# Way down of a feed-forward layer: 8 weight blocks on column parts of 344, or 7 block products on parts of 258

## The chip, the core and the metric

The kernel runs on one core of a Trainium2 chip. The number that counts is device microseconds of one execution. Engines that run beside each other: TensorE (PE, with its weight loads as PEld), VectorE (DVE), ScalarE (ACT), GpSimd (POOL) and SyncE (SP), which here issues nearly all DMAs. Each engine works through its own list of instructions in a fixed order; an instruction that waits holds up all that stand behind it on its engine.

## What is computed

One inference step of a one-layer decoder trunk: a mixer (gated linear attention, a gated recurrence, windowed attention), a cross-attention to a memory, and a feed-forward part. The change touches the feed-forward part alone:

```
D_MODEL = 1024; D_FF = 4096            # tokens: 1024 of the prompt and 8 samples, N = 1032
def ffn(x, g, w1, w2):
    h = rmsnorm(x, g) @ w1             # the way up, 1024 -> 4096
    return jnp.square(jax.nn.relu(h)) @ w2     # the way down, 4096 -> 1024
xp = xp + ffn(xp, g_ffn[l], ffn_w1[l], ffn_w2[l])
```

All is float32. The kernel splits each operand into two rounded halves (hi and lo, type fp32r) and makes each product from three matmuls: hi·hi, hi·lo, lo·hi.

## The kernel before, in words

Tokens lie along the columns, features on the 128 partitions. The 1032 tokens are cut into three groups of 344 columns.

**Block products.** A weight matrix is cut into blocks a11, a12, a21, a22; sums of them are S1 to S4. With matching sums of the operand (T1 to T4 beside B11, B21, B22), seven products of blocks do the work of eight. This holds for two column groups against each other, so groups 0 and 1 go by seven products, and group 2 by the four plain blocks (GA and GB2 are its operand). A unit of work thus has eight steps, one per prepared weight block: A11, S2, S1, A12, S3, S4, A21, A22.

**The way up** (`up_unit`, 14 units; the first 2 of 16 pairs go by `pl_cell`) makes a pair of 128-feature rows of h. `h_done` lists what is then to be done with the pair: sums on DVE and stores (`h_store`) of each operand, split into hi and lo by ACT and DVE (`halves`: ACT rounds, DVE takes the rest), into a place of a ring, from where a DMA carries it to the DRAM tensor `hd[c]`. These entries are run two at a time in the steps of the next unit (`bg_run(2)`). The pairs 0 and 1 are done in the same way out of the list `slow`, one entry in each of the last three steps of a unit.

**The way down** (`down_unit`, 16 units: 8 parts c of 512 features, 2 halves of the outputs each) loads the operands of part c from `hd[c]` by `h_load` into rooms in SBUF. Every product has two row blocks (u), two depths (k) and three terms. Its PSUM result is added by DVE to an accumulator (`add_acc`) and to the output tiles XT (`add`). XT[0] to XT[7] hold the residual x already: `x_fill` loads them from the DRAM tensor `xd` at the start of the way down, after which the first sums can be added. At the end `y_half` transposes XT on PE and ACT copies it out.

**Order.** `prep` makes the weight operand `wop` of the step that is five steps ahead (LOOK), from raw weights `wraw` (`unit_raw`, one unit earlier still) or their sums `wsum` (`unit_sums`, on POOL). A scheduler orders each engine's list by priority: PSUM results (LIFT_E) before weight preparation (LIFT_W) before the rest.

All matmuls stand on line 140 (`mm`), all ACT operations of these stages on 160 (`act`), DVE sums on 170 (`tt`).

Of the kernel before, what the change touches and what calls it, by code (L numbers as in the profile page):

```python
# [52 lines left out]
def trunk_step(ctx: ExitStack, tc: tile.TileContext, I: dict, O: list):  # L53
# [7 lines left out]
    psd = ctx.enter_context(tc.tile_pool(name="psd", bufs=1, space=bass.MemoryType.PSUM))  # L61
# [1807 lines left out]
    hd = [dram.tile([18, 128, 2 * GW], F32, name=f"hd{c}") for c in range(NUNIT)]  # L1869
# [6 lines left out]
    RAW, SUM, OPS = {}, {}, {}  # L1876

# [31 lines left out]
    def prep(q):  # L1909

        n, i = divmod(q, 8)
        if n >= len(UNITS):
            return
        with lift(LIFT_W):
            if i == 0:
# [32 lines left out]
    def h_done(p, h):  # L1948
# [19 lines left out]
    def pl_new(p):  # L1968
        c = cells(T("qe"[p], 6 * GW, "hpl"))
        PL[p] = {(f, g): c[3 * f + g] for f in range(2) for g in range(3)}  # L1970

    XOP = {}

    def up_rooms():
# [4 lines left out]
        HC["g"] = cells(F("g", 4 * GW, "gc"))  # L1979

    def st_rooms():
        HC["h"] = [c for i in range(2) for c in cells(F("u", 3 * GW, "hc"))]
        ST["v"] = F("v", 3584, "wsum")
        room = [F("q", 2064, "hst"), ST["v"][:, 2048:]]
        ST["ring"] = [room[i][:, 2 * GW * j:2 * GW * j + 2 * GW] for i, n in ((0, 3), (1, 2)) for j in range(n)]
# [36 lines left out]
    def up_unit(n):  # L2022
# [9 lines left out]
        for i in range(8):  # L2032
# [54 lines left out]
        bg.extend(h_done(p, h))  # L2087
# [3 lines left out]
    def h_place(c, op):  # L2091
        if c % 2 == 0:
            if op in (B11, GA, B21, GB2):
                k = 2 * (B11, GA, B21, GB2).index(op)
                return XH[:, k:k + 2, gs(0)], XL[:, k:k + 2, gs(0)]
            r = (T2, T1, T3, B22, T4).index(op)
        else:
            if op != B11:
                o = (GA, B21, GB2, T2, T1, T3, B22, T4).index(op)
                k, g = 2 * (o % 4), 1 + o // 4  # L2100
                return XH[:, k:k + 2, gs(g)], XL[:, k:k + 2, gs(g)]
            r = 5
        return [v3(x[r // 3], 6)[:, 2 * (r % 3):2 * (r % 3) + 2] for x in (HOP["hs"], HOP["ls"])]

    def h_load(c, op):
        for s, x in enumerate(h_place(c, op)):
            SP.dma_start(x.bitcast(F32), v3(hd[c][9 * s + op], 2))
        HOP[c, op] = h_place(c, op)

    def x_fill(m):  # L2110

        if m > 3:
            t = v3(F("q", 2 * N, "XT"), 2)
        else:
            t = F("u", N, "XT").unsqueeze(1) if m == 3 else v3(F("v", 3 * N, "XT"), 3)
        for k in range(t.shape[1]):
            XT[m + k] = t[:, k]
            SP.dma_start(XT[m + k], xd[m + k])

    def y_half(m, h):  # L2120
        if "y" not in ST:
            ST["y"], ST["ys"] = F("d", 2048, "yo"), F("u", D, "ys")
        yo = v3(ST["y"][:, m % 2 * 1024 + h * 512:m % 2 * 1024 + h * 512 + 512], 4)
        p = psD("yp")
        for t in range(4):
            tr(p[:, t * 128:(t + 1) * 128], XT[m][:, tok(4 * h + t)])
        act(yo, v3(p, 4), AF.Copy)
        c = slice(m * 128, m * 128 + 128)
        SP.dma_start(y_prompt[0].rearrange("(t p) c -> p t c", p=128)[:, 4 * h:4 * h + 4, c], yo)
        if h == 0:  # L2130
            p = psD("yp")
            tr(p[:8, :128], XT[m][:, :NS])
            ys = ST["ys"][:8, m * 128:m * 128 + 128]
            act(ys, p[:8, :128], AF.Copy)
            SP.dma_start(y_sample.rearrange("b o c -> (b o) c")[:, c], ys)

    def down_unit(n):
        _, c, dq = UNITS[n]
        ps = {}
        first, last = c == 0, c == NUNIT - 1  # L2140
        ms = [[4 * dq + 2 * half + u for u in range(2)] for half in range(2)]
        acc = [HC["g"][2 * dq + u] for u in range(2)]

        def add(m, g, p):
            x = XT[m][:, gs(g)]
            with lift(LIFT_E):
                tt(x, x, p, ADD)

        def add_acc(u, p, new=False):
# [197 lines left out]
```

## Time and profile before

| | |
|---|---|
| median of 3 runs | 1396.75 us (1396.65, 1396.75, 1639.47) |
| profiled execution | 1393.74 us, span 1392.0 us |
| granted TensorE clock | 0.984 of full speed, mean |
| way up (14 units) | about 746 to 1037 us |
| way down (16 units) | 1037 us to the end |
| PE busy over the span | 96% |

Rows of the timeline give the start of an instruction, its length, and how many were merged. Rows of groups give count, busy time, mean length and the idle time before them with what ended it. Matmuls overlap on PE, so what one costs in a stream is the distance from start to start, not its length. Rows of a stretch give busy time and count of each engine, the granted clock, the share of time that the DMA engines were busy, and the GB/s.

### The profile page before, as it was taken

The page shows a single profiled execution, that of the slowest core. Times are in us where ns is not written, and L with a number is a line of the kernel's source. Part 1 is how long each engine was busy: PE and PEld are TensorE (multiplying, and loading weights), DVE is VectorE, ACT ScalarE, POOL GpSimd, SP SyncE. Part 2 cuts the span into 40 slices and gives each one's busy share as a digit, 9 for nine tenths or more (in the row PEclk, how much of TensorE's full clock was granted, in tenths as well). Part 3 has the DMA queues.
Part 4 walks back from the last instruction along what each step waited for, and adds up shares of the span by engine and source line. Part 5 has one row for each costly group of instructions (what it writes and reads, how often), then busy time and mean ns, then how long its engine had stood idle before and what let it go on. Part 6 is the DMA issues. An engine that isn't in the chain of part 4 may idle for free.

```text
span 1392.0 us, 23667 instructions
## 1 busy us (share of the span) xinstructions
PE 1332.0 (96%) x8675; PEld 1226.1 (88%) x8675; DVE 992.3 (71%) x2097; ACT 691.7 (50%) x1439; POOL 260.1 (19%) x245
## 2 busy tenths in 40 slices
PE   6999999999997989998999999999998999999998
PEld 5889888777876877786799999999998999999997
DVE  6276787668767664767698888888766666666674
ACT  5265455245476554555566776766663222222232
POOL 3001011300003101020004232243211321321310
PEclk9999999999998899999999999999999999999999
DMA  6114010211101444442243768766689867655403
GB/s 185 46 49 122 9 49 18 67 26 31 47 8 52 140 146 128 141 133 71 71 125 109 243 223 278 251 236 214 215 308 350 309 218 244 214 188 172 158 17 106
DMA packets 197499, 198.91 MB, mean 143 GB/s; under 512 B 27938, under 2 KB 177558, under 8 KB 197368
## 3 DMA queue, kind: packets, MB, share of 16 engines
q1 hardware_dynamic: 196744, 197.11, 43.7%
q8 instruction: 68, 1.11, 0.3%
q0 software_dynamic: 640, 0.30, 0.1%
q14 instruction: 47, 0.39, 0.1%
HBM read 136.83 MB, written 61.60 MB: 143 GB/s over the span
## 4 chain that ended last, share of the span: by engine, by line
PE 81%; DVE 10%; DMA 3%; ACT 3%; issue 1%; SPq 1%; POOL 1%; DVEq 0%; ACTq 0%; POOLq 0%
PE win L140 9%; PE e L140 9%; PE fe L140 8%; PE wo L140 6%; PE c L140 4%; PE d L140 4%; PE ga L140 4%; PE fa L140 4%; PE fd L140 4%; PE f L140 2%; PE v L140 2%; PE gx L140 2%; PE b L140 2%; PE fb L140 2%; PE fc L140 2%; PE fg L140 2%
## 5 line engine op out<-in xcount | busy, mean ns | idle before, releaser
L1906 POOL TENSOR_TENSOR wsum<-wraw 128x512 f32<-128x512 f32 x60 | 82.4, 1376 | 378.4 <-DVE wop L170 285.7
L140 PE MATMUL e<-XH,wop 128*128 128x344 f32 x512 | 133.3, 322 | 4.4 <-DVE XT L170 4.4
L160 ACT ACTIVATE wop<-wraw 128x512 fp32r<-128x512 f32 x120 | 74.4, 628 | 119.9 <-PE c L140 48.8
L140 PE MATMUL win<-XL,wh 128*128 128x344 f32 x384 | 126.6, 330 | 0.0
L140 PE MATMUL win<-XH,wh 128*128 128x344 f32 x384 | 126.1, 329 | 0.2 <-ACT xy L160 0.2
L140 PE MATMUL win<-XH,wl 128*128 128x344 f32 x384 | 125.5, 327 | 0.0
L160 ACT ACTIVATE wh<-ws 128x512 fp32r<-128x512 f32 x130 | 80.2, 628 | 74.7 <-DMA ws<-in_w_out_dram 21.2
L140 PE MATMUL fe<-XH,wop 128*128 128x344 f32 x448 | 114.7, 319 | 0.0
L170 DVE TENSOR_TENSOR wop<-wraw,wop 128x512 fp32r<-128x512 f32 x120 | 86.5, 721 | 38.1 <-ACT wop L160 37.1
L170 DVE TENSOR_TENSOR wl<-ws,wh 128x512 fp32r<-128x512 f32 x130 | 91.4, 715 | 27.2 <-ACT wh L160 21.8
L160 ACT ACTIVATE wop<-wsum 128x512 fp32r<-128x512 f32 x104 | 65.6, 631 | 84.7 <-PE e L140 59.0
L170 DVE TENSOR_TENSOR wop<-wsum,wop 128x512 fp32r<-128x512 f32 x104 | 74.5, 717 | 40.2 <-ACT wop L160 39.4
L140 PEld LDWEIGHTS e<-XH,wop 128*128 128x128 f32 x512 | 91.5, 190 | 4.7 <-issue 4.7
L140 PE MATMUL e<-XL,wop 128*128 128x344 f32 x256 | 82.5, 322 | 0.0
L140 PEld LDWEIGHTS fe<-XH,wop 128*128 128x128 f32 x448 | 78.9, 188 | 0.0
L140 PEld LDWEIGHTS win<-XL,wh 128*128 128x128 f32 x384 | 72.2, 188 | 5.2 <-issue 3.9
L140 PEld LDWEIGHTS win<-XH,wl 128*128 128x128 f32 x384 | 72.3, 188 | 3.6 <-issue 2.7
L140 PEld LDWEIGHTS win<-XH,wh 128*128 128x128 f32 x384 | 72.2, 188 | 3.3 <-issue 1.9
L140 PE MATMUL fe<-XL,wop 128*128 128x344 f32 x224 | 71.4, 319 | 0.0
L160 ACT ACTIVATE hc<-hc 128x344 f32<-128x344 f32 x126 | 61.4, 488 | 19.5 <-DVE hc L170 18.1
L170 DVE TENSOR_TENSOR hst<-hc,hst 128x344 fp32r<-128x344 f32 x79 | 60.5, 767 | 13.6 <-ACT hst L160 12.4
L140 PE MATMUL wo<-XH,wh 128*128 128x344 f32 x192 | 64.0, 334 | 2.5 <-ACT wh L160 2.5
(537 smaller groups left out, 3916.7 us busy)
## 6 DMA issues: line engine op xcount, KB each, us to landing
hd<-hst SPq DMA_DIRECT2D x90, 344.0 KB
wraw<-in_ffn_w_dram SPq DMA_DIRECT2D x60, 512.0 KB
hd<-wsum SPq DMA_DIRECT2D x54, 344.0 KB
XH<-hd SPq DMA_DIRECT2D x48, 344.0 KB
XL<-hd SPq DMA_DIRECT2D x48, 344.0 KB
xoph<-hd SPq DMA_DIRECT2D x24, 344.0 KB
xopl<-hd SPq DMA_DIRECT2D x24, 344.0 KB
ws<-in_w_in_dram SPq DMA_DIRECT2D x24, 256.0 KB
```

The costliest lines, as they stand in the source:

```text
L140: PE.matmul(out, lhsT, rhs, start=start, stop=stop, **kw)
L160: return ACT.activation(out, in_, func, **kw)
L170: return DVE.tensor_tensor(out, a, b, op=op)
L1906: POOL.tensor_tensor(o, a, b, op=op)
```

## The change

On the way down all 1032 tokens go by seven products, with two halves of 516 columns; each matmul takes a quarter, 258 columns. A unit has seven steps (no A21), of 24 matmuls each. The operands are seven instead of nine, each of 516 columns; they lie in a ring of 12 places (RING), and each `h_load` has a time of its own (`at`). The stores go through three places of 1032 columns instead of five of 688. XT starts from the first products (ACT copies them, `new`), and the residual is loaded to a room that has come free (`x_load`) and added later, a half at a time (`x_add`). On the way down PSUM is one pool of four tiles of two banks. The outputs are transposed by `y_out` in the last unit, copied by ACT and DVE half and half. On the way up the step S3 comes after A21.

```diff
+    first_half = ctx.enter_context(ExitStack())
+    psd = first_half.enter_context(tc.tile_pool(name="psd", bufs=1, space=bass.MemoryType.PSUM))
...
-    A11, S2, S1, A12, S3, S4, A21, A22 = range(8)
-    B11, B21, T2, T1, T3, B22, T4, GA, GB2 = range(9)
+
+    A11, S2, S1, A12, S4, A21, S3, A22 = range(8)
+    B11, T2, B21, T1, T3, B22, T4, GA = range(8)
     NPAIR, NPLAIN, NUNIT = DFF // 256, 2, DFF // 512
+    HALF, QU, NOP = N // 2, N // 4, 7
...
+    hd = [dram.tile([2 * NOP, 128, 2 * HALF], F32, name=f"hd{c}") for c in range(NUNIT)]
...
+    def seq(n):
+
+        if UNITS[n][0] == "up":
+            return range(8)
+        return (A11, S2, A12, S1, S4, S3, A22) if n + 1 == len(UNITS) else (A11, S2, A12, S1, S3, S4, A22)
+
+    QUEUE = [(n, i) for n in range(len(UNITS)) for i in seq(n)]
+    BASE = [QUEUE.index((n, A11)) for n in range(len(UNITS))]
...
-        ring_ = ST["ring"] if p < NPAIR - 1 else ST["ring"][:3]
-        st = ring_[ST["n"] % len(ring_)]
+        st = ST["ring"][ST["n"] % len(ST["ring"])]
         ST["n"] += 1
-        hi, lo = f32r(st[:, :GW]), f32r(st[:, GW:])
+        hi, lo = f32r(st[:, :HALF]), f32r(st[:, HALF:])
...
-        a, b, c, d = h[0, 0], h[0, 1], h[1, 0], h[1, 1]
-        return [st(B11, a), sub(a, b, a), st(GA, h[0, 2]), st(T1, a), sub(b, d, b), st(B22, d), sub(d, d, a), st(T2, d),
-                st(B21, c), sub(c, c, d), st(T3, b), st(GB2, h[1, 2]), st(T4, c)]
+        a, b, c, d = (x[:, i * HALF:(i + 1) * HALF] for x in h for i in range(2))
+        return [st(B11, a), sub(a, b, a), st(T1, a), sub(b, d, b), st(T3, b), st(B22, d), sub(d, d, a), st(T2, d),
+                st(B21, c), sub(c, c, d), st(T4, c)]
...
+        ST["q"] = F("q", 4 * HALF, "hst")
+        ST["ring"] = [ST["q"][:, :N], ST["v"][:, 2048:2048 + N], ST["q"][:, N:]]
...
-                for op in {A12: (B11, GA, B21, GB2, T2, T1, T3, B22), S3: (T4,)}.get(i, ()):
+                for op in {S1: (B11, T2), S4: (B21, T1), S3: (T3, B22)}.get(i, ()):
...
+    RING = (("h", 0, 0), ("h", 0, 1), ("x", 4, 0), ("x", 6, 0), ("h", 1, 0), ("h", 1, 1), ("x", 0, 0), ("x", 2, 0),
+            ("x", 0, 1), ("x", 2, 1), ("x", 4, 1), ("x", 6, 1))
+
+    def h_load(c, op):
...
+        kind, k, j = RING[(NOP * c + op) % len(RING)]
...
+        for s, x in enumerate(room):
+            SP.dma_start(x.bitcast(F32), v3(hd[c][NOP * s + op], 2))
+        HOP[c, op] = room
...
+    def x_load(m):
+
+        ST["x", m] = ST["q"][:, m % 2 * N:m % 2 * N + N]
+        SP.dma_start(ST["x", m], xd[m])
+
+    def x_add(m, j):
+        tt(hv(XT[m], j), hv(XT[m], j), hv(ST["x", m], j), ADD)
...
+    def y_rooms(dq):
...
+            XT[3] = F("u", N, "XT")
+            t = F("v", 3 * N, "XT")
+            for m in range(3):
+                XT[m] = t[:, m * N:(m + 1) * N]
+            t = F("u", N, "acc")
+            HC["acc", 0] = [hv(t, u) for u in range(2)]
...
+    def y_out(m, f):
+
+        p = f("yp")
+        for h in range(2):
+            c = slice(512 * h, 512 * h + 512)
+            for t in range(4):
+                tr(p[:, c][:, t * 128:(t + 1) * 128], XT[m][:, tok(4 * h + t)])
+            yo = ST["q"][:, m % 2 * 1024:m % 2 * 1024 + 1024][:, c]
+            if h == 0:
+                act(yo, p[:, c], AF.Copy)
+            else:
+                copy(yo, p[:, c])
+            SP.dma_start(y_prompt[0].rearrange("(t p) c -> p t c", p=128)[:, 4 * h:4 * h + 4, 128 * m:128 * m + 128],
+                         v3(yo, 4))
...
+        psP, psQ = (lambda name, tag=tag: psy.tile([128, 1024], F32, tag=tag, bufs=2, name=name)
+                    for tag in ("pr" if n % 2 else "rp"))
+
+        def pv(p):
+            return v3(p, 2)[:, :, :QU]
+
+        def add(m, j, p, new=False):
+
+            x = v3(hv(XT[m], j), 2)
             with lift(LIFT_E):
                 if new:
-                    act(acc[u], p, AF.Copy)
+                    act(x, pv(p), AF.Copy)
                 else:
-                    tt(acc[u], acc[u], p, ADD)
+                    tt(x, x, pv(p), ADD)
...
-            terms(ps[name, u], [(hi[:, k, 128 * u:128 * u + 128], lo[:, k, 128 * u:128 * u + 128]) for k in range(2)],
-                  [(f32r(x[0])[:, k], f32r(x[1])[:, k]) for k in range(2)], start, stop)
+            for j in range(2):
+                cs = slice(j * QU, j * QU + QU)
+                terms(ps[name, u][:, 512 * j:512 * j + QU],
+                      [(hi[:, k, 128 * u:128 * u + 128], lo[:, k, 128 * u:128 * u + 128]) for k in range(2)],
+                      [(f32r(x[0])[:, k, cs], f32r(x[1])[:, k, cs]) for k in range(2)], start, stop)
...
-                for u in range(2):
                     add_acc(u, ps["a", u], first)
-                for u in range(2):
-                    part("e", u, GA, True, False)
             elif i == A12:
                 for u in range(2):
                     part("a", u, B21, False, True)
-                for u in range(2):
-                    part("e", u, GB2, False, True)
-                for u in range(2):
-                    add(ms[0][u], 0, ps["a", u])
-                    add(ms[0][u], 2, ps["e", u])
+                    add(ms[0][u], 0, ps["a", u], first)
...
+    def at(n, k, fn):
+        loads.setdefault((n, k), []).append(fn)
+
+    d0 = NPAIR - NPLAIN
+    at(d0, 1, lambda: h_load(0, T4))
+    for c in range(1, NUNIT):
+        for op in range(NOP):
+            n, k = divmod(2 * op + 1, NOP)
+            at(*((d0 + 2 * c - 2 + n, k) if c > 1 else (d0 + 1, op)), lambda c=c, op=op: h_load(c, op))
+    for m in range(8):
+        at(d0 + 3 + m, 0, lambda m=m: x_load(m))
+        for j in range(2):
+            at(d0 + 4 + m, 2 + 3 * j, lambda m=m, j=j: x_add(m, j))
+    psy = None
...
-        c, first = u[1], UNITS[n - 1][1] != u[1] or UNITS[n - 1][0] == "up"
-        if c == 0:
-            for m in (0, 3) if u[2] == 0 else (6,):
-                x_fill(m)
-        if first and c + 1 < NUNIT:
-            for j, op in enumerate((B11, GA, B21, GB2, T2, T1, T3, B22, T4)):
-                loads[8 * n + j + 1] = lambda op=op, c=c: h_load(c + 1, op)
+        if n == d0:
+            first_half.close()
+            psy = ctx.enter_context(tc.tile_pool(name="psy", bufs=1, space=bass.MemoryType.PSUM))
+        if u[1] == 0:
+            y_rooms(u[2])
```

DVE, the sums and stores of a pair in the last unit of the way up (hc is h, hst and wsum the places of the ring, gc and fX are sums and PSUM of that unit). Before:

```order
L170 TENSOR_TENSOR hc<-hc 128x344
L170 TENSOR_TENSOR hst<-hc,hst 128x344 x2
L170 TENSOR_TENSOR wop<-wsum,wop 128x512
L170 TENSOR_TENSOR hst<-hc,hst 128x344
L170 TENSOR_TENSOR wsum<-hc,wsum 128x344
L170 TENSOR_TENSOR hc<-hc 128x344
L170 TENSOR_TENSOR wsum<-hc,wsum 128x344
L170 TENSOR_TENSOR wop<-wraw,wop 128x512
L170 TENSOR_TENSOR gc<-fb,gc 128x344
L170 TENSOR_TENSOR wop<-wraw,wop 128x512
L170 TENSOR_TENSOR gc<-fc,gc 128x344
```

and with the change:

```order
L171 TENSOR_TENSOR hc<-hc 128x516
L171 TENSOR_TENSOR hst<-hc,hst 128x516
L171 TENSOR_TENSOR hc<-hc 128x516
L171 TENSOR_TENSOR wsum<-hc,wsum 128x516
L171 TENSOR_TENSOR hst<-hc,hst 128x516
L171 TENSOR_TENSOR wop<-wsum,wop 128x512
L171 TENSOR_TENSOR gc<-fb,gc 128x344
L171 TENSOR_TENSOR wop<-wraw,wop 128x512
L171 TENSOR_TENSOR gc<-fc,gc 128x344
L171 TENSOR_TENSOR wop<-wraw,wop 128x512
L171 TENSOR_TENSOR wsum<-hc,wsum 128x516
L171 TENSOR_TENSOR hc<-hc 128x516
```

Sums and stores are fewer and wider; what reads PSUM stays as it was.

SP, from the last unit of the way up into the first of the way down (hd_4480 is hd[0], hd_4481 is hd[1], hd_4487 is the last; wraw the weights of the unit after next). Before:

```order
L2107 DMA xopl<-hd_4480 128x688
L1946 DMA hd_4487<-hst 128x2x344
L2107 DMA xoph<-hd_4480 128x688
L2107 DMA xopl<-hd_4480 128x688
L1946 DMA hd_4487<-wsum 128x2x344 x2
L2118 DMA XT<-xd 128x1032 x2
L1946 DMA hd_4487<-hst 128x2x344
L1893 DMA wraw<-in_ffn_w_dram 128x2x512 x2
L1946 DMA hd_4487<-hst 128x2x344 x2
L2107 DMA xoph<-hd_4481 128x688
L2107 DMA xopl<-hd_4481 128x688
L1946 DMA hd_4487<-hst 128x2x344
```

and with the change:

```order
L2117 DMA xoph<-hd_4480 128x1032
L2117 DMA xopl<-hd_4480 128x1032
L2117 DMA xoph<-hd_4480 128x1032
L2117 DMA xopl<-hd_4480 128x1032
L1957 DMA hd_4487<-hst 128x2x516
L1905 DMA wraw<-in_ffn_w_dram 128x2x512 x2
L1957 DMA hd_4487<-wsum 128x2x516
L2117 DMA XH<-hd_4480 128x2x516
L2117 DMA XL<-hd_4480 128x2x516
L1957 DMA hd_4487<-hst 128x2x516 x2
L1957 DMA hd_4487<-wsum 128x2x516
L2117 DMA XH<-hd_4481 128x2x516
```

The loads of part 1 (hd_4481) stand behind the last stores but two instead of among them, and no XT is loaded; the raw weights stand behind the loads of part 0 in both.

ACT, the first unit of the way down, from the results of its first product on. Before:

```order
L160 ACTIVATE gc<-ga 128x344 x2
L160 ACTIVATE wop<-wraw 128x512 x3
L160 ACTIVATE hst<-hc 128x344
L160 ACTIVATE wop<-wsum 128x512 x2
L160 ACTIVATE hst<-hc 128x344 x2
L160 ACTIVATE wop<-wraw 128x512
L160 ACTIVATE wop<-wsum 128x512
L160 ACTIVATE hst<-hc 128x344
```

and with the change:

```order
L161 ACTIVATE gc<-a 128x516 x2
L161 ACTIVATE wop<-wraw 128x512
L161 ACTIVATE hst<-hc 128x516
L161 ACTIVATE wop<-wraw 128x512
L161 ACTIVATE XT<-a 128x516 x2
L161 ACTIVATE wop<-wsum 128x512
L161 ACTIVATE XT<-c 128x516 x2
L161 ACTIVATE wop<-wraw 128x512
L161 ACTIVATE hst<-hc 128x516
L161 ACTIVATE wop<-wsum 128x512
L161 ACTIVATE XT<-c 128x516
```

Between the weight preparations there are now copies of PSUM (XT<-a, XT<-c) that were sums on DVE before.

## Rows read from the trace of the kernel before

**Rows 1.** page, part 1: engine, busy us (share of the span), instructions

```profile
PE 1332.0 (96%) x8675; PEld 1226.1 (88%) x8675; DVE 992.3 (71%) x2097; ACT 691.7 (50%) x1439; POOL 260.1 (19%) x245
```

**Rows 2.** stretches: one unit of the way up, one of the way down

```profile
833.00:853.80 20.80, 20.80 (x134) 20.80 (x133) 17.69 (x30) 14.12 (x32) 6.01 (x4) 1.00 0.87 284
...
1181.20:1202.10 20.90, 20.90 (x134) 20.79 (x133) 14.20 (x28) 5.08 (x8) 5.55 (x4) 1.00 0.38 123
```

**Rows 3.** chain that ended last: start, length, what

```profile
1038.94 1.90 PE e L140 x12
...
1059.85 1.92 PE e L140 x12
1066.98 7.65 DMA XT<-xd
...
1086.70 1.91 PE e L140 x12
...
1212.05 1.90 PE e L140 x12
...
1295.62 1.90 PE e L140 x12
```

**Rows 4.** stretches around that wait (columns as in Rows 2)

```profile
1070.00:1075.00 5.00, 1.32 (x9) 1.02 (x7) 1.73 (x3) 0.79 (x2) 0.00 (x0) 1.00 1.04 399
1075.00:1080.00 5.00, 4.27 (x19) 4.30 (x20) 3.40 (x8) 0.00 (x0) 0.00 (x0) 0.66 1.04 399
```

**Rows 5.** timeline of PE: matmuls of 256 columns in a stream

```profile
120.75 0.40 PE L140 MATMUL mkv<-mhl,wh 128*128 128x256 f32 x2
...
126.44 0.40 PE L140 MATMUL mkv<-mhl,wh 128*128 128x256 f32 x2
...
171.99 0.28 PE L140 MATMUL v<-wh,XL 128*128 128x256 f32 x1
...
173.78 0.29 PE L140 MATMUL v<-wh,XL 128*128 128x256 f32 x1
```

**Rows 6.** groups of DVE on the way up, 746 to 1037 us

```profile
L170 DVE TENSOR_TENSOR hst<-hc,hst 128x344 fp32r<-128x344 f32 x72 | 54.4, 756 | 12.3 <-ACT hst L160 11.1
L170 DVE TENSOR_TENSOR hc<-hc 128x344 f32<-128x344 f32 x54 | 44.6, 825 | 1.2 <-ACT hc L160 0.5
L170 DVE TENSOR_TENSOR wop<-wsum,wop 128x512 fp32r<-128x512 f32 x57 | 42.0, 739 | 15.6 <-ACT wop L160 15.3
L170 DVE TENSOR_TENSOR wop<-wraw,wop 128x512 fp32r<-128x512 f32 x56 | 41.7, 744 | 4.7 <-ACT wop L160 4.1
L170 DVE TENSOR_TENSOR wsum<-hc,wsum 128x344 fp32r<-128x344 f32 x47 | 28.5, 606 | 9.5 <-ACT wsum L160 8.9
L170 DVE TENSOR_TENSOR hc<-fd,gc 128x344 f32<-128x344 f32 x28 | 14.3, 510 | 0.2 <-PE fd L140 0.2
```

**Rows 7.** groups of DVE in one unit of the way down

```profile
L170 DVE TENSOR_TENSOR wop<-wsum,wop 128x512 fp32r<-128x512 f32 x4 | 2.8, 692 | 1.8 <-ACT wop L160 1.8
```

**Rows 8.** waits on the way up, 746 to 1037 us: total, times, longest

```profile
ACT hst L160 <- DMA hd<-hst: 6.4, 5, 1.5
ACT wsum L160 <- DMA hd<-wsum: 5.2, 3, 3.4
```

**Rows 9.** waits at the start of the way down, 1037 to 1100 us

```profile
PE e L140 <- DVE XT L170: 4.4, 1, 4.4
...
ACT hst L160 <- DMA hd<-hst: 3.3, 4, 1.6
DVE XT L170 <- DMA XT<-xd: 2.9, 4, 1.9
```

**Rows 10.** stretch of the first unit of the way down (columns as in Rows 2)

```profile
1037.00:1057.00 20.00, 20.00 (x128) 19.89 (x127) 15.20 (x27) 9.14 (x18) 4.34 (x5) 1.00 0.96 339
```

**Rows 11.** timeline of ACT and SP at the end

```profile
1386.98 1.08 ACT L160 ACTIVATE yo<-yp 128x512 f32<-128x512 f32 x2 [0.60 <-PE yp L146]
...
1387.60 0.92 SPq L2129 DMA_DIRECT2D out_dram<-yo  x2
```

More of the change, by code (lines that the diff above doesn't have):

```diff
@@ L2105, in h_load @@
[L2105 to L2113, printed above, removed]
-        else:
[L2115 to L2135, printed above, removed]
@@ new lines, in hv @@
+    def hv(x, j):
+        return x[:, j * HALF:(j + 1) * HALF]
+    def x_load(m):
[4 more added lines that the diff above has]
+    def y_rooms(dq):
+        if dq:
+            for m in (4, 6):
+                t = F("q", 2 * N, "XT")
+                XT[m], XT[m + 1] = t[:, :N], t[:, N:]
+            HC["acc", 1] = [HC["gt"][:, u * HALF:(u + 1) * HALF] for u in range(2)]
+        else:
+            XT[3] = F("u", N, "XT")
[4 more added lines that the diff above has]
+            HC["acc", 0] = [hv(t, u) for u in range(2)]
@@ L2137, in down_unit, with ys_out @@
+    def ys_out(ms, f):
+        p = f("ysp")
+        n = 128 * len(ms)
+        for i, m in enumerate(ms):
+            tr(p[:8, i * 128:i * 128 + 128], XT[m][:, :NS])
+        ys = HC["gt"][:8, :n] if ms[0] == 0 else HC["gt"][:8, 1032:1032 + n]
+        act(ys, p[:8, :n], AF.Copy)
+        SP.dma_start(y_sample.rearrange("b o c -> (b o) c")[:, 128 * ms[0]:128 * ms[0] + n], ys)
     def down_unit(n):
@@ L2139, in down_unit @@
         ps = {}
-        first, last = c == 0, c == NUNIT - 1
+        first, last, end = c == 0, c == NUNIT - 1, n + 1 == len(UNITS)
         ms = [[4 * dq + 2 * half + u for u in range(2)] for half in range(2)]
[L2142 to L2149, printed above, removed]
+        acc = HC["acc", dq]
+        psP, psQ = (lambda name, tag=tag: psy.tile([128, 1024], F32, tag=tag, bufs=2, name=name)
+                    for tag in ("pr" if n % 2 else "rp"))
@@ L2150, in add_acc @@
+        def pv(p):
+            return v3(p, 2)[:, :, :QU]
+        def add(m, j, p, new=False):
+            x = v3(hv(XT[m], j), 2)
             with lift(LIFT_E):
                 if new:
-                    act(acc[u], p, AF.Copy)
+                    act(x, pv(p), AF.Copy)
                 else:
-                    tt(acc[u], acc[u], p, ADD)
+                    tt(x, x, pv(p), ADD)
+        def add_acc(u, p, new=False):
+            a = v3(acc[u], 2)
+            with lift(LIFT_E):
+                if new:
+                    act(a, pv(p), AF.Copy)
+                else:
+                    tt(a, a, pv(p), ADD)
@@ L2161, in banks @@
         def banks(f, name):
             for u in range(2):
-                ps[name, u] = f(name)[:, :GW]
-        for i in range(8):
-            q = 8 * n + i
+                ps[name, u] = f(name)
+        for k, i in enumerate(seq(n)):
+            q = BASE[n] + k
             prep(q + LOOK)
             bg_run(2)
-            load = loads.get(n * 8 + i)
-            if load:
-                load()
+            for fn in loads.get((n, k), ()):
+                fn()
             hi, lo = OPS.pop(q)
@@ L2185, in down_unit @@
                     part("a", u, B21, False, True)
-                for u in range(2):
-                    part("e", u, GB2, False, True)
-                for u in range(2):
-                    add(ms[0][u], 0, ps["a", u])
-                    add(ms[0][u], 2, ps["e", u])
+                    add(ms[0][u], 0, ps["a", u], first)
+                if end:
+                    for m in (0, 1):
+                        y_out(m, psP)
             elif i == S2:
-                banks(psD, "b")
+                banks(psQ, "b")
                 for u in range(2):
@@ L2196, in down_unit @@
                     if last:
-                        for m, g in ((ms[0][u], 1), (ms[1][u], 0), (ms[1][u], 1)):
-                            add(m, g, acc[u])
+                        for m, j in ((ms[0][u], 1), (ms[1][u], 0), (ms[1][u], 1)):
+                            with lift(LIFT_E):
+                                tt(hv(XT[m], j), hv(XT[m], j), acc[u], ADD)
+                if end:
+                    for m in (2, 3):
+                        y_out(m, psQ)
             elif i == S1:
-                banks(psD, "c")
+                banks(psQ, "c")
                 for u in range(2):
                     part("c", u, T1, True, False)
-                    add(ms[1][u], 1, ps["c", u])
+                    add(ms[1][u], 1, ps["c", u], first)
             elif i == S3:
-                banks(psC, "d")
+                banks(psP, "d")
                 for u in range(2):
@@ L2211, in down_unit @@
                     part("c", u, B22, False, True)
-                    add(ms[0][u], 1, ps["c", u])
-            elif i == A21:
-                banks(psB, "e")
-                for u in range(2):
-                    part("e", u, GA, True, False)
-                for m in ms[0] * last:
-                    y_half(m, 0)
-                    y_half(m, 1)
+                    add(ms[0][u], 1, ps["c", u], first)
+                if end:
+                    for m in ms[0]:
+                        y_out(m, psQ)
+                    ys_out(range(6), psQ)
             else:
@@ L2222, in down_unit @@
                     part("d", u, T4, False, True)
-                    add(ms[1][u], 0, ps["d", u])
-                for u in range(2):
-                    part("e", u, GB2, False, True)
-                    add(ms[1][u], 2, ps["e", u])
-                    if last:
-                        y_half(ms[1][u], 0)
-        for m in ms[1] * last:
-            y_half(m, 1)
+                    add(ms[1][u], 0, ps["d", u], first)
+                if end:
+                    for m in ms[1]:
+                        y_out(m, psP)
+                    ys_out(range(6, 8), psQ)
     def w1_blk(f):
@@ L2303, in trunk_step @@
     run_steps()
-    slow.extend(h_done(0, PL[0]) + h_done(1, PL[1]))
+    slow.extend(h_done(0, PL["t", 0]) + h_done(1, PL["t", 1]))
+    def at(n, k, fn):
[11 more added lines that the diff above has]
+    psy = None
     for n, u in enumerate(UNITS):
```

43 lines of the change are left out of this document (15 added, 28 removed).

## The prediction

> **What bounds the kernel.** I read the page's busy shares first: PE works through 96% of the span, DVE through 71% [rows 1]. The share alone would not do, so I took stretches of one unit each. On the way up and on the way down PE is busy without a gap and at full clock, while DVE has 17.7 of 20.8 us on the way up and 14.2 of 20.9 on the way down, ACT 14.1 and 5.1 [rows 2]. So each unit lasts as long as its matmuls. The chain of waits gives the period of a down unit: the same product starts at 1212.05 and, four units later, at 1295.62, which is 20.89 us [rows 3]. A unit has 132 matmuls of 344 columns (11 products of 12), so one costs 158.3 ns. The one break is early: between 1059.85 and 1086.70 the chain needs 26.85 us for one unit, 5.96 more than the period, and the step in between is the load of XT [rows 3]. PE stood 4.4 us for a sum on DVE that waited for that load [rows 9], and after it the granted clock of a 5 us stretch was 0.66, that is, a part of it at 1.2 instead of 2.4 GHz [rows 4].
>
> **The matmuls.** The change takes out 132 matmuls of 344 columns a unit and puts in 7 × 24 = 168 of 258. By columns that is 43,344 for 45,408, only 4.5% less, so everything hangs on what a narrower matmul costs. The kernel has streams of 256 columns, with a weight load for each matmul as here: 48 in 5.69 us from 120.75 to 126.44, that is 118.5 ns, and 15 in 1.79 us, that is 119.3 [rows 5]. From 256 to 344 columns a column costs (158.3 − 118.9)/88 = 0.45 ns, so two more make 119.8; I take 120.0. Bounds: 118.7 if cost goes with columns (158.3 × 258/344), 122.5 if all above the bare column time at 2.4 GHz (158.3 − 143.3 = 15.0) is fixed per matmul. A unit becomes 168 × 120.0 = 20.16 us and 16 units give back 16 × (20.89 − 20.16) = **11.7 us** (5 to 15.2). The gain is gone at 20.89/168 = 124.3 ns.
>
> **The load of XT.** It is no longer waited for: ACT copies the first products into XT, and the residual is added in units 4 to 11 of the way down, when nothing waits for it. That gives back the excess of **6.0 us**. The sums of the residual are two of 516 columns a unit, about 0.7 us each; with 7 splits and 14 sums of PSUM DVE then has 7 × 0.69 + 16 × 0.70 = 16.0 of 20.2 us, so PE hides them.
>
> **What comes late instead.** Two places at the start of the way down are close. (a) Four loads of part 0 can't be issued before the fifth product of the last up unit is done with their rooms, 84 of its 132 matmuls or 13.3 us into it. Behind them on SP and in the DMA queue stand a store, four more loads, a store, and then the raw weights of the unit after next: 10 × 0.528 + 1.05 = 6.3 MB. A full queue moved 339 to 399 GB/s [rows 4, 10], so they land 16 to 19 us later, 8 to 11 us into the first down unit. ACT's list has the rounding of these weights ahead of its copy of the third product (XT<-a), whose banks the fifth needs at 4 × 24 × 0.120 = 11.5 us. (b) The loads of T4 come after that, 1.6 MB and 4 to 5 us later, 12 to 16 us into the unit; they are needed at 17.3, and PE's list puts half a product of the next unit ahead. One unit later the raw weights stand behind the last stores, again about as early as needed. I take **1 us** for all this; nothing below, 8 us above (the old wait again with its clock, and a little more). The loads of part 1, which filled the queue at the old wait, now have a unit to themselves.
>
> **The way up.** Its matmuls stay. DVE gets 11 sums and stores of 516 for 13 of 344, ACT 7 roundings for 9. A sum that reads PSUM, which nothing disturbs, takes 510 ns for 344 columns [rows 6] and a split of 512 takes 692 [rows 7], so one of 516 is about 0.70: 11 × 0.70 − 13 × 0.51 = 1.1 us more per unit, and 22 × 0.70 − 26 × 0.51 = 2.1 us once for the pairs in the list `slow`. DVE has 3.1 us of idle time per unit to hide it; if that cover were gone, each us would be one of PE. The ring has three places for five. For the last pair the old kernel used three as well, with the DMA queue full, and ACT waited 3.3 us for it in all [rows 9], against 11.6 us over the whole way up with five [rows 8]. ACT is idle 6.7 us a unit, and weights are made five steps ahead, so a wait of that size is hidden. I take **1 us** for the way up; bounds 0 and 30, the latter below.
>
> **The end.** Before and after, 72 transposes stand between the last products, and the path behind the last matmul is a sum, transposes, a copy, a DMA of 256 KB [rows 11]. The sum is 0.2 us longer, one of the two copies goes to DVE, and in the last unit transposes wait for banks that DVE frees after six sums of 0.7 us. I take **0.5 us**, bounds −1 and 2.
>
> **Sum.** 1393.74 − 11.7 − 6.0 + 1 + 1 + 0.5 = 1378.5 us for the profiled execution. The two runs that agree, the median one among them, lie 3.0 us above it, so I forecast **1381 us**, 1.1% less than before.
>
> **Rivals.**
> - *DVE bounds the way up (slower).* For: its sums of two SBUF operands take 606 to 825 ns against 510 with a PSUM operand [rows 6], at the times when POOL works on its sums. If the disturbed lengths grow with the columns, 173 such entries at 127.5 us in all become 1.5 × 11/13 of that, 34 us more over 14 units, and `slow` 4 more. Of the 43 us idle, 39 are waits for ACT (11.1, 15.3, 4.1 and 8.9 [rows 6]), which stay. Then some 34 us come through: 1381 − 1 + 34 = 1414 us. It decides once the extra work of a unit passes the 0.3 us that is truly free. Against: these waits for ACT stand where DVE is ahead of its work, and shrink when it falls behind. Chance 0.06. The Trainium skill, "SBUF — State Buffer", section "Who interferes with whom", says that a DVE instruction with two SBUF inputs and a GpSimd one that reads SBUF exclude each other for their whole length; by that rule the wait goes with POOL's instructions, which the change leaves alone, and the rival falls away. The trace agrees in that only those with two SBUF operands are long (825 against 510 ns).
> - *A new wait at the start of the way down.* If (a) or (b) comes 3 us later than I work out, PE stops, and the clock falls as it did before [rows 4]: 6 to 8 us, 1387 to 1389. Chance 0.10.
> - *The change doesn't do what it says.* At 124.3 ns or more for a matmul of 258 columns, since two streams into two banks and 36 more weight loads a unit are new: 1393 and up. Against it stand rows of 118.5 and 119.3 ns for nearly that width. Chance 0.04.
> - *The bare column time.* If the 15 ns above the columns were not paid in this stage, 258 columns would cost 107.5 ns, a unit 18.06 us, and 16 units 45 us less than before: 1381 − 34 = 1347. The rows speak against it: at 256 columns 12 ns remain. Chance 0.02. The Trainium skill, "TensorE: Matmul & The Clock Gate", section "Back-to-back issue gap", gives N/2.4 + 2.5 ns for a warm matmul by itself, an estimate of 110 ns here and about 1354 us. By that rule 344 columns would take 146 ns; the trace has 158.3, so the measurement decides.
>
> The forecast has 0.78. **Range** 1372 to 1394: it takes in the bounds of the matmul's price (3.5 us less to 6.7 more), the new wait, and the case of no gain where that begins; it leaves out most of the DVE rival and the bare column time, 0.06 + 0.02, and some 0.1 of the edges. **Chances**: 2% is about what a measurement of this kernel can tell from no change; faster by more needs less than 1368.8, which the bare column time and a sliver of the forecast give: 0.03. Slower by more needs over 1424.7, the DVE rival at its worst: 0.02. Within: 0.95.
>
> **What would show it.** Right: twelve matmuls of 258 columns in 1.44 us; a down period of 20.2 us; no wait of PE for XT, and the residual's loads far from the chain; an up period of 20.8 us still. Wrong: 1.49 us or more for twelve; DVE over 20 us in an up unit with PE waiting for its sums (gc<-fb, hc<-fd); PE idle 10 to 20 us into the way down with ACT or DVE held by a DMA; a stretch there at a lower clock.

## The result, and the profile after

The changed kernel takes **1405.69 us** (median of 5 runs, 1404.23 to 1409.29) against 1396.65 for the kernel before on the same chip: a ratio of 1.0086, 95% interval 1.0059 to 1.0114. (One run of the kernel before, of 1639.47 us, was in a slower state; the ratio leaves it out.) The change makes the kernel 0.9% slower. The forecast was 1381 us, range 1372 to 1394: wrong in sign, and outside its range.

The page's first part of the changed kernel, to set beside [rows 1]:

```profile
PE 1326.3 (94%) x9251; PEld 1219.1 (87%) x9251; DVE 1017.0 (72%) x1993; ACT 686.8 (49%) x1393; POOL 255.1 (18%) x245
```

Shares of the whole span hide what happened. Two stretches show it, one unit of the way up and one of the way down (start and end, length, busy time and count of PE, PEld, DVE, ACT, POOL, granted clock, DMA share, GB/s), to set beside [rows 2]:

```profile
790.70:813.30 22.60, 21.10 (x133) 20.81 (x133) 18.72 (x28) 15.33 (x31) 5.95 (x4) 1.00 0.71 258
1110.20:1130.40 20.20, 20.20 (x171) 20.20 (x170) 13.98 (x20) 4.92 (x8) 5.35 (x5) 1.00 1.04 397
```

The way down is as forecast: a unit in 20.2 us, PE without a gap. The way up is not: its unit is now 22.6 us, and PE is idle in 1.5 of them.

The chain of waits of the changed kernel gives both periods: `fd` is A22's first product on the way up, `a` a product of the way down.

```profile
768.25 2.15 PE fd L141 x12
...
790.24 0.44 DVE hc L171
790.72 2.16 PE fd L141 x12
...
812.80 0.44 DVE hc L171
813.28 2.15 PE fd L141 x12
...
1110.24 2.87 PE a L141 x24
...
1130.37 2.86 PE a L141 x24
...
1150.50 2.88 PE a L141 x24
```

From 1110.24 to 1150.50 two units take 40.26 us, that is 20.13 for one and 119.8 ns for a matmul of 258 columns; I had 20.16 and 120.0. From 790.72 to 813.28 an up unit takes 22.56 us for 20.81 before, and a DVE instruction stands in the chain just ahead of each `fd`. The waits of PE between 748 and 1072 us (total, times, longest):

```profile
PE fd L141 <- DVE hc L171: 22.1, 13, 3.7
PE a L141 <- ACT hc L161: 0.5, 1, 0.5
```

In the kernel before PE waited for nothing between 746 and 1037 us, and between 1037 and 1100 for XT alone [rows 9]. Its stretch from 748 to 1036 us has PE busy all the time:

```profile
748.00:1036.00 288.00, 288.00 (x1829) 288.00 (x1828) 239.00 (x381) 198.69 (x426) 85.32 (x58) 1.00 0.68 232
```

The account of the profiled executions goes by the first matmul of the way up and of the way down. Before:

```profile
745.50 0.32 PE L140 MATMUL fa<-XH,wop 128*128 128x344 f32 x1
...
1036.89 0.32 PE L140 MATMUL ga<-XH,wop 128*128 128x344 f32 x1
```

and with the change:

```profile
748.72 0.32 PE L141 MATMUL fa<-XH,wop 128*128 128x344 f32 x1
...
1069.64 0.39 PE L141 MATMUL a<-xoph,wop 128*128 128x258 f32 x1 [0.55 <-ACT hc L161]
```

Up to the way up it is +3.2 us, with the same work, which is the distance of one execution from another; the way up takes 320.9 us for 291.4, **+29.5**; the way down 337.7 us for 355.1, **−17.4**. Together that is +15.3, from 1392.0 to 1407.3. (The profiled execution of the changed kernel is the slowest of its five, so the medians lie only 9 us apart.) Of the 29.5 us, 22.6 are the waits above; the rest, some 7 us, is a lower clock after two of them and about 0.26 us a unit that do not show as waits (a unit with a wait of 1.39 us takes 22.46 for 20.81).

One of the thirteen places, in the timeline of the changed kernel (in brackets the idle time before, and what ended it):

```profile
785.31 0.69 DVE L171 TENSOR_TENSOR wop<-wsum,wop 128x512 fp32r<-128x512 f32 x1
...
787.45 1.62 POOL L1918 TENSOR_TENSOR wsum<-wsum,wraw 128x512 f32<-128x512 f32 x1
...
787.85 1.78 DVE L171 TENSOR_TENSOR wop<-wraw,wop 128x512 fp32r<-128x512 f32 x1
...
788.06 0.32 PE L141 MATMUL fd<-xoph,wop 128*128 128x344 f32 x1
...
789.01 0.32 PE L141 MATMUL fe<-XH,wop 128*128 128x344 f32 x1
...
789.55 0.68 DVE L171 TENSOR_TENSOR hpl<-hpl 128x516 f32<-128x516 f32 x1
790.16 0.50 DVE L171 TENSOR_TENSOR hc<-fd,gc 128x344 f32<-128x344 f32 x1
...
790.72 0.43 PE L141 MATMUL fd<-XH,wop 128*128 128x344 f32 x1 [1.39 <-DVE hc L171]
```

S3's product into the bank fd ends at 788.06 + 0.32 us. The next product into the same bank is A22's, and it may begin only when DVE has read S3's result (`hc<-fd,gc`). PE's list has six matmuls to fe in between, 0.95 us, and then PE stands. DVE has two instructions ahead of the read: a split of 512 columns that takes 1.78 us, while GpSimd sums, instead of 0.69 as two lines up, and a difference of 516 columns. So the read ends 2.34 us after the product (0.95 + 1.39). In the kernel before, S4 and A21 stood between S3 and A22; its chain of waits has them as 24 matmuls:

```profile
757.04 1.89 PE fd L140 x12
758.93 1.89 PE fg L140 x12
760.81 1.88 PE fe L140 x12
762.69 1.90 PE fd L140 x12
```

There the read had 3.76 us, from 758.93 to 762.69. Twice the clock fell after the wait as well. After 2.35 us of idle time (before 859.16) and after 3.65 (before 952.85) the 20 us stretch has a granted clock of 0.91, part of it at 1.2 instead of 2.4 GHz; after waits of 1.39 it stays at 1.00:

```profile
840.00:860.00 20.00, 17.65 (x112) 17.36 (x111) 16.60 (x25) 13.91 (x29) 4.34 (x4) 1.00 0.79 275
860.00:880.00 20.00, 20.00 (x119) 20.00 (x118) 13.51 (x21) 12.66 (x26) 4.12 (x4) 0.91 0.66 237
...
940.00:960.00 20.00, 16.35 (x95) 16.06 (x94) 13.97 (x21) 10.66 (x24) 7.49 (x5) 0.91 0.48 172
960.00:980.00 20.00, 18.61 (x118) 18.32 (x118) 15.38 (x22) 11.66 (x24) 5.83 (x4) 1.00 0.65 234
```

### The profile page after: what moved, and what is told of

It is laid out like the page before. It is cut to its first block, busy times and chain, and to the rows that moved or that the text cites. A ratio compares the mean times of both kernels' runs of the same rounds, so it can differ in the third digit from the quotient of the medians.

```text
span 1407.3 us, 24488 instructions
## 1 busy us (share of the span) xinstructions
PE 1326.3 (94%) x9251; PEld 1219.1 (87%) x9251; DVE 1017.0 (72%) x1993; ACT 686.8 (49%) x1393; POOL 255.1 (18%) x245
## 4 chain that ended last, share of the span: by engine, by line
PE 73%; DVE 14%; ACT 5%; DMA 3%; issue 3%; SPq 1%; POOL 0%; DVEq 0%; ACTq 0%; POOLq 0%
PE win L141 9%; PE a L141 7%; PE d L141 7%; PE c L141 7%; PE wo L141 6%; PE fe L141 4%; PE b L141 3%; PE fa L141 3%; PE fd L141 2%; PE v L141 2%; PE f L141 2%; PE gx L141 2%; PE fb L141 2%; PE fc L141 2%; PE wmo L141 2%
## 5 line engine op out<-in xcount | busy, mean ns | idle before, releaser
L161 ACT ACTIVATE wop<-wraw 128x512 fp32r<-128x512 f32 x104 | 65.3, 628 | 118.5 <-PE b L141 31.3
L171 DVE TENSOR_TENSOR wop<-wraw,wop 128x512 fp32r<-128x512 f32 x104 | 93.5, 899 | 27.8 <-ACT wop L161 24.7
L171 DVE TENSOR_TENSOR wop<-wsum,wop 128x512 fp32r<-128x512 f32 x104 | 80.7, 776 | 17.4 <-ACT wop L161 15.0
L141 PE MATMUL a<-XH,wop 128*128 128x258 f32 x352 | 67.6, 283 | 0.0
L141 PE MATMUL wo<-XH,wl 128*128 128x344 f32 x192 | 64.1, 334 | 1.0 <-DVE wl L171 0.9
L141 PE MATMUL wo<-XL,wh 128*128 128x344 f32 x192 | 63.0, 328 | 0.0
L141 PE MATMUL d<-XH,wop 128*128 128x258 f32 x320 | 60.8, 282 | 0.0
```

The lines of the kernel that those rows point to most:

```text
L141: PE.matmul(out, lhsT, rhs, start=start, stop=stop, **kw)
L161: return ACT.activation(out, in_, func, **kw)
L171: return DVE.tensor_tensor(out, a, b, op=op)
```

## Experiments

The theory (A): the new place of S3 next to A22 makes PE wait for DVE's read of fd. The rivals: (B) DVE has too much to do, in any order; (C) the ring of three places holds ACT and so DVE; and later (E) GpSimd's hold on DVE, (F) the width of 516 itself. All ratios are to the kernel before, run on the same chip.

**1. The changed kernel with the old up order.**

```diff
         if UNITS[n][0] == "up":
-            return range(8)
+            return (A11, S2, S1, A12, S3, S4, A21, A22)
...
-                for op in {S1: (B11, T2), S4: (B21, T1), S3: (T3, B22)}.get(i, ()):
+                for op in {S1: (B11, T2), S4: (B21, T1, T3, B22)}.get(i, ()):
```

> The changed kernel with the order of the eight products on the way up as it was before (S3, S4, A21, A22 at its end; the first four late loads of part 0 all issued after S4). Theory A, the order: in the changed kernel A22 follows S3 directly and adds to the bank fd that DVE has not yet read, so PE waits 1.4 to 3.7 us in each of 13 units (22.1 us) and the clock falls in two of them; the way up took 320.8 us for 291.2. With the old order 24 matmuls stand between, the up period is 20.8 us again, the way up 291 to 293 us, and the time 1405.7 - 29 = 1376 to 1379 us. Theory B, the amount of work on DVE: the wider sums and stores and the ring of three places make DVE late in any order; PE then waits at some other product, the way up stays over 305 us and the time over 1390 us.

1391.19 us, ratio 0.9965 (0.9951 to 0.9979). The way up takes 302.0 us: 19 of the 29.5 are gone, 10.6 stay. Neither forecast holds alone. (Here S3 overwrites a part of T4's operand before it is stored: the first 516 columns of the lower row reach into the 344 that S3 writes. The order of the change writes them later; run 5 stores them earlier.)

**2. The kernel before with the new up order alone** (steps S4, A21, S3, A22; T3's operand is overwritten before its store).

```diff
+    UP = (A11, S2, S1, A12, S4, A21, S3, A22)
...
-        for i in range(8):
-            q = 8 * n + i
+        for j, i in enumerate(UP):
+            q = 8 * n + j
```

> The kernel before with only the new order of the products on the way up (S4, A21, S3, A22 at its end); sums, stores, ring and the whole way down stay. Theory A, the order: the waits of fd for DVE come here too, 12 to 14 of them, 1 to 2 us each, and the time rises by 15 to 30 us to 1412 to 1427 us. Theory B, the amount of work on DVE: narrower sums and a ring of five leave DVE in time, no wait of PE at fd over 0.3 us, and the time stays at 1393 to 1400 us.

1416.44 us, ratio 1.0155 (1.0138 to 1.0172): theory A. Stores of 344 columns and a ring of five do not save it. The waits of PE between 748 and 1050 us:

```profile
PE fd L140 <- DVE hc L170: 14.2, 12, 1.7
```

A thirteenth, of 1.18 us, ends at 1052.37, still on the way up, which takes 310.5 us, 19.1 more than before.

**3. The changed kernel, A22 adding to fe first.**

```diff
-                terms(ps["fd"], w, XOP[T4], False, True)
                 terms(ps["fe"], w, XOP[GA][4:], False, True)
+                terms(ps["fd"], w, XOP[T4], False, True)
```

> The changed kernel, but A22 adds its twelve products to fe ahead of its twelve to fd. That leaves the order of the eight steps and every operation, and puts 1.89 us of matmuls between S3's product and the bank fd's next use. Theory A, the order: the waits of 1.4 to 2.3 us shrink to 0 to 0.5 us each and the clock does not fall; the way up takes 292 to 298 us for 320.8, the time is 1377 to 1384 us. Theory B, the amount of work on DVE: DVE stays late, PE waits elsewhere (gc<-fb, hc<-fg or in the next unit), time over 1395 us.

1394.61 us, ratio 0.9994 (0.9982 to 1.0006). Twelve matmuls now cover the read, 1.89 us, and the shortest waits fall from 1.39 to 0.45 us: 1.89 + 0.45 is 2.34 again, the time that DVE needs. The forecast of 0 to 0.5 us holds for 6 of the 12; the others last 0.7 to 1.9:

```profile
PE fd L141 <- DVE hc L171: 9.3, 12, 1.9
```

After the longest of them, 1.93 us, the clock falls (0.66 in the next 5 us). The way up takes 307.9 us, 13 less than with the change but more than the 292 to 298 that theory A gave, and the time lies above its 1377 to 1384: twelve matmuls are too little cover. Theory B fails too: behind 748 us PE waits nowhere else but for 2.28 us ahead of the first product of the way down.

**4. The changed kernel without GpSimd's block sums on the way up.**

```diff
+        if UNITS[n][0] == "up":
+            SUM[n] = {S1: a21, S2: a11, S3: a11, S4: a12, A11: a11, ...}
+            return
```

> The changed kernel without GpSimd's four sums of weight blocks in each unit of the way up (left out: S1 to S4 use blocks of W1 as they are). The order stays. In the trace of the changed kernel DVE's split of 512 columns just ahead of the read of fd takes 1.78 us instead of 0.67 while GpSimd sums. Theory A in its plain form, the order and one split and one difference that DVE's list has ahead of the read: with the split at 0.67 us each wait is 1.1 us shorter, 0.3 to 0.8 us a unit is left, and the way up takes 295 to 303 us. Theory A', it is the dependency alone (matmul end, signal, read, signal): the waits stay at 1.4 us. Theory C, GpSimd's hold on DVE is the whole cause: no wait is left, 291 to 293 us.

1380.47 us in one run. Of the gain 9 us lie ahead of the way up, whose first matmul comes at 739.4 us for 748.7; run 9, with the same edit, has it at 746.2, so this part is not shown to come from the edit. PE's waits on the way up are two, for 13, with the order as it was changed:

```profile
PE fd L141 <- DVE hc L171: 4.0, 2, 2.1
```

The way up takes 301.6 us, in theory A's range of 295 to 303, but not in the way that it said. The units without a wait take 20.89 to 21.06 us, 0.1 to 0.25 more than before, so each loses less than A's 0.3 to 0.8. The rest is in the two waits, 1.83 and 2.14 us, and the lower clock after each (0.66 in the next 5 us). The second falls beside GpSimd's sums for the way down, which this run keeps; the first begins about 8 us after a row of four of them, and what held DVE there is not shown.

So the order alone costs little in most units: it takes away the cover, and GpSimd's sum, which makes the split ahead of the read 1.1 us longer, makes that felt in nearly every unit.

**5. The old order, with the pair's stores done by the fifth step.** Run 1 and

```diff
-            bg_run(2)
+            bg_run(3 if k == 4 else 2)
```

> The changed kernel with the old order of the products on the way up, and the last of the eleven sums and stores of the pair before run at the fifth step, ahead of S3's new sum (in the order that the change replaced, the 516 columns of the lower row hold half of what S3 writes, so they have to be stored before it). Theory A, the order is two thirds of the loss and the rest is something else: as the run with the old order alone, 1387 to 1392 us, with 3 to 6 waits of PE left. Theory B, the old order without that detail was what was still slow: 1377 to 1381 us.

1388.47 us, ratio 0.9957 (0.9942 to 0.9972), faster than both kernels, with six waits of PE left on the way up: theory A. The way up takes 301.2 us. With runs 1 and 2 that makes a square: old order and stores of 344 columns 291.4 us; new order alone +19.1; the 516 columns and their ring alone +9.8; both +29.5. The two add up. What the 9.8 are, the next runs ask. In this kernel PE waits six times on the way up, 6.2 us, and 1.9 at the first product of the way down:

```profile
PE fd L141 <- DVE hc L171: 5.2, 5, 1.7
PE a L141 <- ACT hc L161: 1.9, 1, 1.9
PE fg L141 <- DVE gc L171: 1.0, 1, 1.0
```

The worst place, DVE and GpSimd from 924 us on:

```profile
924.28 1.76 POOL L1918 TENSOR_TENSOR wsum<-wraw 128x512 f32<-128x512 f32 x1
...
924.91 1.69 DVE L171 TENSOR_TENSOR hc<-hc 128x516 f32<-128x516 f32 x1
...
926.00 1.75 POOL L1918 TENSOR_TENSOR MKV<-wraw,wsum 128x512 f32<-128x512 f32 x1
...
926.52 1.79 DVE L171 TENSOR_TENSOR hst<-hc,hst 128x516 fp32r<-128x516 f32 x1
...
927.70 1.76 POOL L1918 TENSOR_TENSOR wsum<-wraw,wsum 128x512 f32<-128x512 f32 x1
...
928.23 1.78 DVE L171 TENSOR_TENSOR wsum<-hc,wsum 128x516 fp32r<-128x516 f32 x1
...
929.93 0.68 DVE L171 TENSOR_TENSOR wop<-wraw,wop 128x512 fp32r<-128x512 f32 x1
```

In this row each DVE instruction with two operands in SBUF lasts about as long as one of GpSimd's; once GpSimd is done, 0.68 us. `MKV` belongs to the first unit of the way down: its sums had come forward to here.

**6. Five places in the ring, old order.**

```diff
+        more = F("q", 4 * HALF, "hst")
-        ST["ring"] = [ST["q"][:, :N], ST["v"][:, 2048:2048 + N], ST["q"][:, N:]]
+        ST["ring"] = [ST["q"][:, :N], ST["v"][:, 2048:2048 + N], ST["q"][:, N:], more[:, :N], more[:, N:]]
```

> The kernel of the old order and early stores with five places of 1032 columns in the ring for the stores, where the change has three (the room of a residual tile that nothing uses then). With three places and the old order ACT waited 22.1 us for stores to land on the way up, against 11.6 in the kernel before, and PE four times (6.9 us) between 850 and 940 us, when DMA was busy 0.77 to 0.84 of the time. Theory C, the ring holds what is left: ACT waits under 5 us, PE's waits from 748 to 1036 us go, 6.9 us of them and about 2 us of lower clock, 1379 to 1383 us. Theory D, DVE's own amount of work holds it: ACT waits less but PE's waits stay, 1387 to 1392 us.

1394.18 us, ratio 0.9997 (0.9984 to 1.0009). ACT's waits for stores fall from 26.8 us (run 5, on the way up) to 2.9, and the way up from 301.2 to 300.4 us: theory C falls. PE still waits three times there, 4.1 us in all, and after the longest of these, 1.93 us, the clock falls (0.66 in the next 5 us). The whole got slower than in run 5 because the new places lie where XT begins later, so that ACT's first copy into XT waits for the last stores to land:

```profile
1067.38 1.09 ACT L161 ACTIVATE XT<-c 128x516 f32<-128x516 f32 x2 [6.57 <-DMA hd<-hst]
...
1068.04 0.58 PE L141 MATMUL c<-xoph,wop 128*128 128x258 f32 x1 [8.41 <-ACT XT L161]
```

**7. The same, the first product of the way down in other banks.**

```diff
+            psy.tile([128, 1024], F32, tag="p", bufs=2, name="first")
```

> As the run with five places, and the first product of the way down is moved to the other four banks of PSUM. In the old order PE waited 2.3 us for ACT's read of the last fe before the first product of the way down, and the clock of the next 5 us was 0.66. If the bank is what it waits for, this wait goes: 3 to 4 us less than with five places alone, 1375 to 1380 us. If another wait stands there at once (DVE's read of the last fd, or an operand's load), no change.

1396.23 us, ratio 1.0003 (0.9988 to 1.0017); the wait of that product is 1.92 us as in run 6. Whether the edit moved it to other banks is not shown, so this is inconclusive.

**8. Five places in the changed kernel's own order** (the edit of run 6).

> The changed kernel in its own order with five places in the ring. Theory A, in this order the wait is for DVE's read of fd and the ring has no part in it (ACT waited only 3.7 us for stores): within 2 us of the changed kernel, 1403 to 1408 us, 12 to 14 waits at fd. Theory C, the ring makes DVE late there too: 1385 to 1398 us.

1422.63 us, ratio 1.0194 (1.0175 to 1.0213), slower than either theory gave. A wait of 8.1 us for XT's place comes here as well, and at fd PE waits 22.2 us in 11 places; the way up takes 325.1 us for 320.9. More room in the ring does not shorten the waits, as theory A said.

**9. Run 5 without GpSimd's sums on the way up** (the edit of run 4).

> The kernel of the old order and early stores, without GpSimd's sums of weight blocks on the way up (left out: S1 to S4 use blocks of W1 as they are). In its trace with the sums PE waits six times for DVE between 825 and 937 us (6.2 us) and 1.9 us at the first product of the way down; around 921 to 930 us five of GpSimd's sums stand in a row, and each of DVE's instructions with two operands in SBUF takes 1.7 to 1.8 us for 0.69. Theory E, GpSimd's hold on DVE is what is left of the loss: all six waits go, the way up takes 291 to 294 us for 301.2. Theory F, the 516 columns themselves make DVE late: 298 to 301 us.

The way up takes 293.5 us, and of all waits the one at the first product of the way down is left, 1.92 us. Theory E; the width of 516 by itself costs nothing that PE sees on the way up (1380.65 us in one run). With runs 4 and 5 this makes a second square: the new order costs 19.7 us of the way up beside GpSimd's sums (320.9 for 301.2) and 8.1 without them (301.6 for 293.5). So a good half of the order's cost comes only with GpSimd (by one execution of each kernel).

**10. Run 5, the last stores four a step.**

```diff
-            bg_run(3 if k == 4 else 2)
+            bg_run(4 if n == NPAIR - NPLAIN - 1 else 3 if k == 4 else 2)
```

> The kernel of the old order and early stores, with the stores of the last but one pair run four a step in the last up unit, so that they are done three steps earlier. If the first product of the way down waits 1.9 us because ACT's read of the last fe is queued behind a store whose sum on DVE is late, this wait and about 1.5 us of lower clock after it go: 1384 to 1387 us. If GpSimd's first sums for the way down hold DVE there, no change, 1387 to 1390 us.

1389.19 us, ratio 0.9965 (0.9955 to 0.9976), with the same wait of 1.92 us: not the stores.

**11. Run 5, block sums of the up units on DVE.**

```diff
-            POOL.tensor_tensor(o, a, b, op=op)
+            if n < NPAIR - NPLAIN:
+                tt(o, a, b, op)
+            else:
+                POOL.tensor_tensor(o, a, b, op=op)
```

> The kernel of the old order and early stores, with the four sums of weight blocks of each up unit on DVE and not on GpSimd. That gives DVE 4 x 0.68 = 2.7 us more a unit and takes GpSimd's four instructions of 1.3 to 1.8 us away. Theory E, GpSimd's hold on DVE: the waits between 825 and 937 us go, the way up takes 292 to 296 us, the time is 1379 to 1384 us. Theory F, DVE has too much work: PE's waits grow, the way up takes 303 us or more, 1390 us or more.

**1377.56 us**, ratio 0.9885 (0.9870 to 0.9900), a little below theory E's 1379 to 1384. The stretch from 748 to 1036 us, first of run 5, then of this run:

```profile
748.00:1036.00 288.00, 281.81 (x1780) 280.26 (x1779) 236.66 (x340) 193.21 (x386) 84.65 (x55) 1.00 0.69 241
```

```profile
748.00:1036.00 288.00, 286.91 (x1820) 286.63 (x1818) 245.56 (x397) 202.90 (x396) 11.49 (x7) 1.00 0.73 253
```

DVE is busy 9 us longer, and PE waits for it no more on the way up, which takes 293.5 us, as in run 9. What made DVE late was not how much it had to do (theories B and F) but that GpSimd's sums stopped it at the wrong moments (E).

**12. The same for the first two units of the way down as well, with the edit of run 10.**

```diff
-            if n < NPAIR - NPLAIN:
+            if n < NPAIR - NPLAIN + 2:
```

> As the run with the sums on DVE, also for the first two units of the way down, and with the early last stores. Theory E: also the 1.9 us at the first product of the way down and its lower clock go, 2 to 4 us less than with the sums on DVE for the way up alone: 1376 to 1381 us. If that product waits for the banks in any case: as that run.

**1375.17 us**, ratio 0.9872 (0.9859 to 0.9886): the lowest, though its interval overlaps with that of run 11, and by the ratios some 30 us below the changed kernel. The way up takes 292.3 us. The wait at the first product of the way down is not gone, as theory E had it, but is 0.79 us for 1.92, and the clock of the next 5 us is 1.00 for 0.66:

```profile
PE a L141 <- ACT hc L161: 0.8, 1, 0.8
```

## Why the prediction was wrong

**The step that failed** is the way up: "Its matmuls stay", and with them, I took it, its 20.8 us a unit, with 1 us in all for DVE, ACT and the ring. It measured +29.5 us. That this lies just inside the bounds that I had given (0 and 30) is luck: the 30 came from the rival below, whose mechanism is another. The text on the change says that S3 comes after A21, and the prediction never priced it, though the matmuls staying does not make their dependences stay: I looked at how long DVE was busy, and not at how long each of its reads may take before the same bank is needed again. That time fell from 24 matmuls to 6, from 3.76 to 0.95 us, for a read that ends 2.34 us after the product. The rows of before would have told a part of it: a read of 0.51 us [rows 6] behind one split of 0.69 [rows 7] needs 1.2 us, 0.25 more than 0.95, which is about what a unit loses in run 4; the rest comes with GpSimd's hold on the split. Runs 2 and 5 size the two parts: 19 us the order, 10 us the 516 columns, each beside GpSimd's sums. Without these sums (runs 4 and 9) they are 8.1 and 2.1 us.

**The matmuls: right.** 119.8 ns for 258 columns, forecast 120.0; 16 × (20.89 − 20.13) = 12.2 us for 11.7. The estimate of 110 ns from the Trainium skill, "TensorE: Matmul & The Clock Gate", section "Back-to-back issue gap", is not what these streams show; the section gives it for a matmul by itself.

**The load of XT: right.** No wait of PE for XT is left, −6.0 us. **What comes late, and the end: right in size.** The whole way down gave 17.4 us; beside 12.2 and 6.0 that leaves a cost of 0.8, for 1.5 forecast, as a remainder that no run measures by itself. Neither (a) nor (b) stopped PE.

**The rival "DVE bounds the way up"** had the right stage, sign and culprit, and the wrong mechanism. It asked whether DVE's work fills the unit; it doesn't: run 11 has the busiest DVE, and no wait of PE for it. It also let GpSimd's disturbance grow with the columns. The rows of one sum, the rest that a store keeps beside its rounded half, in the kernel before and in the changed one, 748 to 1036 us (shortest, median and longest in ns):

```profile
L170 DVE TENSOR_TENSOR hst<-hc,hst x72: 502/518/1636, 756.7 to 1035.4; 128x344 fp32r<-128x344 f32 x72
```

```profile
L171 DVE TENSOR_TENSOR hst<-hc,hst x55: 678/696/1826, 764.4 to 1033.7; 128x516 fp32r<-128x516 f32 x55
```

From median to longest is 1.12 us for 344 columns and 1.13 for 516: the longest hold is the same for both widths. The Trainium skill, "SBUF — State Buffer", section "Who interferes with whom", says that the shared port pair is an exclusive lock, taken for a whole instruction. These rows agree: GpSimd's sums are 512 columns wide in both kernels, and DVE's reads of PSUM stay at 0.50 to 0.52 us. But I drew from that rule that the rival "falls away", since GpSimd's work stays as it was. The hold was no larger; it only met a place without cover.

**The ring: right.** With five places the way up gains 0.8 us in the old order (run 6) and nothing in the new one (run 8).

**Not settled:** why the first product of the way down waits 1.92 us in the old order (0.55 in the changed kernel). Runs 7 and 10 left it as it was, and run 12 more than halved it; that GpSimd's first sums for the way down hold DVE there fits, and isn't shown apart from that.

## What to carry to other kernels

When a change reorders products, ask for each PSUM bank how many matmuls stand between the last write and the next one, and what the reading engine's list has ahead of the read at that time; DVE's busy share (17.7 of 20.8 us here) said nothing on it. An engine that is merely helped by GpSimd may be better off without the help: here four sums of 0.69 us on DVE cost less than four of GpSimd's that stop DVE for up to 1.1 us each. And where a stage was bound by its matmuls, a price per matmul from a neighbouring width of the same trace was good to 1% here; the dependences are what had to be looked for.

## What the runs showed of the hardware

In a row of five sums on GpSimd, DVE's instructions with two operands in SBUF went from 0.69 us each to between 1.69 and 1.81 (run 5, from 921 us on). GpSimd pays too: its sum of 512 columns takes 1.29 us at its shortest and 1.63 to 1.76 in that row. In the changed kernel PE's clock stayed at 1.00 through ten waits of 1.4 to 1.5 us each and fell after single ones of 2.35 and 3.65. The length of a wait alone does not tell, though: after one of 2.13 us (before 1066.17) the next 5 us are at 1.00, and in run 5 after one of 1.92 us (before 1046.83) at 0.66.
